# One conditioning load for each weight unit of the first SwiGLU, and the last vector's reduction near that SwiGLU's end

## The chip, the core and the metric

The kernel runs on one core of a Trainium2 chip. Time is device time of one launch in microseconds (us), and the median of the runs is compared. PE stands for the matmul engine (TensorE), DVE for VectorE, ACT for ScalarE, POOL for GpSimd, and SP for SyncE, whose queue issues all the loads here.

## What is computed

One decoder layer on 512 positions of width 1024, in fp32: a SwiGLU feed-forward (half step), a token mixer, a second SwiGLU, and a final norm. Each of the three sub-layers is conditioned: nine vectors of 1024 numbers (shift, scale and gate, three times) come from one small product of a vector `c` with a large matrix. Cut to what matters:

```python
c_act = jax.nn.silu(c)                                        # 1024
mod = (c_act @ w_ada[l] + b_ada[l]).reshape(B, 9, D_MODEL)    # w_ada: 1024 x 9216
sh1, sc1, gt1, sh2, sc2, gt2, sh3, sc3, gt3 = ...             # the nine vectors
h = _modulate(_rmsnorm(x, g_ffn1[l]), sh1, sc1)
x = x + MACARON_W * gt1 * _swiglu(h, w1_gate[l], w1_up[l], w1_down[l])
h = _modulate(_rmsnorm(x, g_mix[l]), sh2, sc2)
x = x + gt2 * _hybrid_mixer(h, ...)
h = _modulate(_rmsnorm(x, g_ffn2[l]), sh3, sc3)
x = x + MACARON_W * gt3 * _swiglu(h, w2_gate[l], w2_up[l], w2_down[l])
return _rmsnorm(x, g_final)
```

## The kernel before, in words

**Weights.** All large weights are cut into units of up to 128 x 1024 numbers (512 KB). The first SwiGLU has 68 of them (`n_ffn`): units 0 to 7 hold the first columns of gate and up, 8 to 23 and 35 to 56 the rest, 24 to 34 and 57 to 67 the two halves of down. `load_unit` (L352) loads a unit into one of four `raw` buffers from the SP queue (L356). `make_units` (L372) has ACT write its rounded part `whi` (L378), and `low_part` (L364) has DVE or POOL write the remainder `wlo` (L367) and gives the `raw` buffer back, so that the next load can go. There are four pairs of `whi` and `wlo`, and two more pairs for the last two units of a SwiGLU (`KEEP`; `whik`, `wlok` in the trace). The event `loaded[u]` is set with a unit's load, `made[u]` with its `wlo`. Each product is three matmuls, hi times hi, hi times lo and lo times hi, so a unit of eight 128 x 128 blocks is 24 matmuls of 512 columns. All of them go through the helper at L286.

**Conditioning.** The first two vectors are worked out ahead of the SwiGLU. The other seven, in the order 2, 4, 3, 5, 7, 6, 8, are worked out beside it. Each takes eight loads of 512 KB (`ada_loads`, L857, issued at L861 into one of three `araw` buffers), 56 in all. DVE multiplies each loaded tile by one column of the activated `c` and adds it to the vector's partial sums `ada` (`ada_sums`, L865; the first of eight at L875, the other seven at L878). `ada_reduce` (L885) then adds over partitions: four short matmuls on PE (L891, in the trace eight records under L286 with `ada`), a copy by ACT (L896), two transposes on PE (L899), and one or two short operations on DVE into `mod` and `am` (L902 to L912). The reduction of a vector is put in after the fourth sum of the next one (`LATER` is 3). The last vector has no next one, so its reduction comes right behind its last sum.

**Order.** A planner (`Plan`, L137) fixes the order of all instructions of every engine ahead of time. It keeps a modelled time for each engine and for the DMA queue; a step becomes ready when the events and buffers that it asks for are there in that modelled time, and the step that can start first goes first, ranks breaking ties. Each engine, and SP's queue, then runs its list strictly in that order, and waits at an instruction whose operands or buffers aren't there. The conditioning's loads and sums have rank `R_ADA` (4), the units' loads `R_LOAD` (1). The conditioning's loads ask for a free `araw` buffer and nothing else, so the planner issues the next one as soon as a sum has freed one. `glu` (L605) makes the SwiGLU's products: silu by ACT (L608), a product by DVE (L612), a rounded copy by ACT (L617), the remainder by DVE (L619). `first_half` (L638) adds the first half of down to `x`, with the gate (vector 2), at L640; `rope_tables` (L917) follows vector 4.

Of the kernel before, what the change touches and what calls it, by code (L numbers as in the profile page):

```python
# [22 lines left out]
DK = D // P  # L23
# [50 lines left out]
A_ACT = 3  # L74
HOLD = 0
N_AW = 3
LATER = 3
KEEP = (2, 2, 0)
N_PT = 4
R_H0 = 0.4  # L80
# [12 lines left out]
R_NORM, R_X, R_H, R_GLU, R_A0, R_LOAD, R_W, R_ADA, R_TAB, R_MAIN = 0, 0.5, 0.6, 0.7, 1, 2, 3, 4, 5, 9  # L93
# [43 lines left out]
class Plan:  # L137
# [12 lines left out]
    def go(self, rank, task):  # L150
        self.n += 1
        self.step([rank, self.n, task, [self.at], None], None)
# [8 lines left out]
    def give(self, slots, i, at=None):  # L161
        slots.idle.append((*(at or self.at), i))
        able = [w for w in slots.waiters if w[4] < len(slots.idle)]
        if able:
            w = min(able, key=lambda w: w[:2])
            slots.waiters.remove(w)
            self.step(w, self.take(slots, w))
# [52 lines left out]
def c_act(n):  # L220
    return ACT, 0.1 + 0.84e-3 * n
# [6 lines left out]
def c_stt(n):  # L228
    return DVE, 0.13 + 1.04e-3 * n


def c_ts(n):
    return DVE, 0.12 + 0.55e-3 * n
# [14 lines left out]
def c_dma(n):  # L248

    return DMA, max(0.05, n * 0.356e-3)  # L250
# [6 lines left out]
def tile_hymba_layer(ctx: ExitStack, tc: tile.TileContext, xT, pos, cols_d, con_d, wa0, wa1, f1a, f1b, f1d,  # L257
# [6 lines left out]
    go, give, done = plan.go, plan.give, plan.set  # L264
# [20 lines left out]
    def mm(o, lhsT, rhs, start, stop):  # L285
        nc.tensor.matmul(o, lhsT, rhs, start=start, stop=stop)  # L286
# [15 lines left out]
    def cv(n, i=0, w=1):  # L302
        a = _COLS[n][0] + i
        return col[:, a:a + w]

    def kv(n, i=0, w=None):
        a, full = _CON[n]
        return con[:, a + i:a + i + (full if w is None else w)]
# [12 lines left out]
    n_ffn = len(units)  # L321
# [20 lines left out]
    loaded, made = [Event() for _ in units], [Event() for _ in units]  # L342
# [514 lines left out]
    def ada_loads():  # L857
        for n in range(7 * DK):
            i = yield aws
            yield c_dma(4 * D)  # L860
            nc.sync.dma_start(aw[i], wa1[n // DK, n % DK])  # L861
            aw_at[n] = i
            done(aw_in[n])

    def ada_sums():  # L865
        summed = []
        for n in range(7 * DK):
            i, k = divmod(n, DK)
            yield aw_in[n]
            if k == 0:  # L870
                j = yield adas
            a, w = ada[j], aw[aw_at[n]]
            if k == 0:
                yield c_ts(D)
                nc.vector.tensor_scalar(a, w, cact[:, 0:1], None, op0=OP.mult)  # L875
            else:
                yield c_stt(D)
                nc.vector.scalar_tensor_tensor(a, w, cact[:, k:k + 1], a, op0=OP.mult, op1=OP.add)  # L878
            give(aws, aw_at[n])
            if k == DK - 1:  # L880
                summed.append((order[i], j))
            if summed and (k == LATER or n == 7 * DK - 1):
                go(R_ADA, ada_reduce(*summed.pop()))

    def ada_reduce(m, j):  # L885

        b = yield banks
        pc = bank_of[b]
        yield PE, 0.59
        for r in range(4):  # L890
            mm(pc[32 * r:32 * r + 32, :256], kv("ones"), ada[j][:, 256 * r:256 * r + 256], True, True)  # L891
        give(adas, j)
        q = yield scr
        yield c_act(256)
        t = scr_of[q]
        nc.scalar.activation(t[:, :256], pc[:, :256], AF.Copy)  # L896
        yield PE, 0.22
        for i in range(2):
            nc.tensor.transpose(pc[:, (2 + i) * P:(3 + i) * P], t[:, i * P:(i + 1) * P], ident)  # L899
        give(scr, q)  # L900
        yield SMALL
        nc.vector.tensor_add(mod[:, m].rearrange("p (r i) -> p r i", i=2),  # L902
                             pc[:, 2 * P:].rearrange("p (i r n) -> p r i n", i=2, r=4)[:, :, :, 0],
                             cv("b", m * 8, 8).rearrange("p (r i) -> p r i", i=2))
        give(banks, b)
        s, r = divmod(m, 3)
        if r == 1:
            yield SMALL
            nc.vector.scalar_tensor_tensor(am[:, s], mod[:, m], 1.0, cv(g8[s], 0, 8), op0=OP.add, op1=OP.mult)
        elif r == 2 and s != 1:  # L910
            yield SMALL
            nc.vector.tensor_scalar(mod[:, m], mod[:, m], 0.5, None, op0=OP.mult)  # L912
        done(mod_in[m])
# [51 lines left out]
    with tc.tile_pool(name="g0", bufs=1) as gp:  # L965
        go(R_ADA, ada_loads())
        go(R_ADA, ada_sums())
        go(R_TAB, rope_tables())
        parts = start_builds(1, norm)
        ffn(0, gp, accs, norm, end)  # L970
        plan.run(end)
        plan.run(mod_in[8])
        plan.run(tables_in)
# [3 lines left out]
    with ExitStack() as mixer:  # L977
# [505 lines left out]
        summed = [0] * 4  # L1483
# [134 lines left out]
        n = 0  # L1618
# [296 lines left out]
```

## Time and profile before

| | |
|---|---|
| median of 3 runs | 1060.53 us (1058.64 to 1061.17) |
| the profiled execution | 1059.17 us, of it the span 1057.4 us |
| PE busy | 1024.0 us, 97% of the span |
| DVE, ACT, POOL busy | 607.2, 409.0, 62.7 us |
| mean granted TensorE clock | 0.988 of full speed |
| HBM read | 130.14 MB, 125 GB/s over the span |

The first SwiGLU takes from about 60 us to 420 us of the span, the mixer to about 690 us, the second SwiGLU the rest. A row of the timeline gives the start, the time, the engine, the line and the operation of one instruction, and in square brackets the idle time of its engine before it and what ended that.

### The profile page before, as it was taken

Reading aid. Unit: us, or ns where it says so; the run is one execution under the profiler, and the core shown is the slowest. Engines: PE = TensorE matmul, PEld = TensorE weight load, DVE = VectorE, ACT = ScalarE, POOL = GpSimd, SP = SyncE. Lnnn points to the kernel's source line nnn. Section 1 sums busy time; section 2 is a strip of 40 time slices with the busy share of each in tenths; the row PEclk is TensorE's granted clock in tenths of the full one; section 3 lists DMA queues with packets and bytes.
Section 4 is the critical chain, followed back from the end, with each engine's and each line's share of the span. In section 5 each row is a group of like instructions: output and inputs, shape, how many; then the busy total and the mean of one; then the engine's idle time right before and its main releaser. Section 6 shows DMA issues by size and latency. Waiting matters only on the chain.

```text
span 1057.4 us, 13873 instructions
## 1 busy us (share of the span) xinstructions
PE 1024.0 (97%) x5409; PEld 859.6 (81%) x5409; DVE 607.2 (57%) x1064; ACT 409.0 (39%) x719; POOL 62.7 (6%) x52
## 2 busy tenths in 40 slices
PE   8999899899999999999999999999999999999997
PEld 5778677588888889997778778998888888888887
DVE  4988788743333345499889996654333323333334
ACT  4552222122222232356868985434322222222321
POOL 0310010000000002011121110100000000000000
PEclk8999999899999999999999999999999999999998
DMA  9659889522222230233510003224233333323202
GB/s 333 264 190 332 311 307 311 199 96 100 100 100 100 94 116 20 99 112 105 200 37 29 13 14 113 79 83 135 90 94 97 100 100 99 99 90 93 98 20 80
DMA packets 40706, 133.60 MB, mean 126 GB/s; under 512 B 4704, under 2 KB 8032, under 8 KB 40000
## 3 DMA queue, kind: packets, MB, share of 16 engines
q1 hardware_dynamic: 40640, 132.71, 37.0%
q8 instruction: 42, 0.69, 0.3%
q14 instruction: 24, 0.20, 0.1%
HBM read 130.14 MB, written 2.10 MB: 125 GB/s over the span
## 4 chain that ended last, share of the span: by engine, by line
PE 73%; DVE 13%; DMA 9%; issue 2%; ACT 2%; SPq 0%; DVEq 0%; ACTq 0%
PE b L286 71%; DMA araw<-in_wa_dram 8%; DVE ada L878 3%; DVE wlo L367 1%; DVE PT L1427 1%; PE b L1416 1%; DVE afirst L748 1%; DMA wfirst<-in_wa_dram 1%; DVE P L1344 1%; DVE s L531 1%; ACT whi L378 0%; DMA raw<-in_f1b_dram 0%; DVE q L1108 0%; DVE s L1058 0%; DVE s L612 0%
## 5 line engine op out<-in xcount | busy, mean ns | idle before, releaser
L286 PE MATMUL b<-hhi,whi 128*128 128x512 f32 (+1 forms) x1020 | 380.8, 373 | 1.4 <-DVE pc L1267 1.3
L286 PE MATMUL b<-hlo,whi 128*128 128x512 f32 (+1 forms) x1020 | 376.0, 369 | 0.8 <-DVE hlo L537 0.4
L286 PE MATMUL b<-hhi,wlo 128*128 128x512 f32 (+1 forms) x1020 | 375.5, 368 | 0.0
L378 ACT ACTIVATE whi<-raw 128x1024 fp32r<-128x1024 f32 (+3 forms) x176 | 177.9, 1012 | 444.2 <-PE b L286 296.9
L367 DVE TENSOR_TENSOR wlo<-raw,whi 128x1024 fp32r<-128x1024 f32 (+3 forms) x157 | 185.4, 1181 | 213.9 <-ACT whi L378 212.8
L286 PEld LDWEIGHTS b<-hhi,whi 128*128 128x128 f32 x1020 | 193.2, 189 | 35.3 <-issue 3.5
L286 PEld LDWEIGHTS b<-hhi,wlo 128*128 128x128 f32 x1020 | 193.2, 189 | 32.1
L286 PEld LDWEIGHTS b<-hlo,whi 128*128 128x128 f32 x1020 | 193.3, 189 | 31.5 <-DVE hlo L537 1.3
L286 PE MATMUL b<-ghi,whi 128*128 128x512 f32 (+1 forms) x364 | 137.1, 377 | 0.0
L286 PE MATMUL b<-glo,whi 128*128 128x512 f32 (+1 forms) x364 | 136.3, 374 | 0.4 <-DVE glo L619 0.4
L286 PE MATMUL b<-ghi,wlo 128*128 128x512 f32 (+1 forms) x364 | 136.2, 374 | 0.0
L612 DVE TENSOR_TENSOR s<-sg,b 128x512 f32<-128x512 f32 x44 | 30.1, 686 | 101.4 <-PE b L286 100.7
L878 DVE SCALAR_TENSOR_TENSOR ada<-araw,cact,ada 128x1024 f32<-128x1024 f32 x49 | 69.6, 1420 | 20.0 <-DMA araw<-in_wa_dram 19.6
L286 PEld LDWEIGHTS b<-ghi,whi 128*128 128x128 f32 x364 | 68.8, 189 | 13.6 <-issue 1.6
L286 PEld LDWEIGHTS b<-glo,whi 128*128 128x128 f32 x364 | 68.8, 189 | 12.8 <-DVE glo L619 0.8
L286 PEld LDWEIGHTS b<-ghi,wlo 128*128 128x128 f32 x364 | 68.8, 189 | 12.1
L367 POOL TENSOR_TENSOR wlo<-raw,whi 128x1024 fp32r<-128x1024 f32 (+2 forms) x19 | 43.9, 2311 | 286.8 <-ACT whi L378 260.7
L544 DVE SCALAR_TENSOR_TENSOR x<-b,mod,x 128x512 f32<-128x512 f32 (+1 forms) x30 | 19.1, 643 | 41.0 <-PE b L286 40.9
L462 ACT ACTIVATE s<-x 128x256 f32<-128x256 f32 (+1 forms) x41 | 19.4, 491 | 55.5 <-DVE x L544 53.7
L617 ACT ACTIVATE ghi<-s 128x512 fp32r<-128x512 f32 x44 | 27.6, 631 | 30.3 <-DVE s L612 30.3
L535 ACT ACTIVATE hhi<-s,mod 128x256 fp32r<-128x256 f32 (+1 forms) x42 | 20.9, 534 | 32.5 <-DVE s L531 29.4
L1427 DVE TENSOR_TENSOR PT<-b,PT 128x384 fp32r<-128x384 f32 (+1 forms) x48 | 28.0, 595 | 3.8 <-ACT PT L1425 3.6
(241 smaller groups left out, 963.9 us busy)
## 6 DMA issues: line engine op xcount, KB each, us to landing
araw<-in_wa_dram SPq DMA_DIRECT2D x56, 512.0 KB
raw<-in_f1b_dram SPq DMA_DIRECT2D x38, 512.0 KB
raw<-in_f2b_dram SPq DMA_DIRECT2D x38, 512.0 KB
raw<-in_f1d_dram SPq DMA_DIRECT2D x22, 512.0 KB
raw<-in_f2d_dram SPq DMA_DIRECT2D x22, 512.0 KB
raw<-in_wib_dram SPq DMA_DIRECT2D x14, 512.0 KB
wfirst<-in_wa_dram SPq DMA_DIRECT2D x5, 1024.0 KB
raw<-in_wc_dram SPq DMA_DIRECT2D x8, 512.0 KB
```

The source lines that it names most:

```text
L286: nc.tensor.matmul(o, lhsT, rhs, start=start, stop=stop)
L367: (nc.vector if e == DVE else nc.gpsimd).tensor_sub(wlo_of[j][:, :n], raw_of[i][:, :n], whi_of[j][:, :n].bitcast(F32))
L378: nc.scalar.activation(whi_of[j][:, :n], raw_of[raw_at[u]][:, :n], AF.Copy)
L462: nc.scalar.activation(o[:, ts], x[d][:, ts], AF.Square)
L531: nc.vector.scalar_tensor_tensor(t, x[d][:, ts], am[:, s, d:d + 1], rb(), op0=OP.mult, op1=OP.mult)
L535: nc.scalar.activation(hhi[d][:, ts], t, AF.Identity, bias=sh)
L544: nc.vector.scalar_tensor_tensor(x[d][:, ts], bank_of[b][:, ts], gate, x[d][:, ts], op0=OP.mult, op1=OP.add)
L612: nc.vector.tensor_mul(scr_of[q], sg_of[k], bank_of[bu])
L617: nc.scalar.activation(ghi[j], scr_of[q], AF.Copy)
L748: nc.vector.scalar_tensor_tensor(a[:, 0], w[:, k], cact[:, k:k + 1], a[:, 0], op0=OP.mult, op1=OP.add)
L878: nc.vector.scalar_tensor_tensor(a, w, cact[:, k:k + 1], a, op0=OP.mult, op1=OP.add)
L1427: nc.vector.tensor_sub(pl[:, :w], pt[:, :w], ph[:, :w].bitcast(F32))
```

## The change

The loads of the conditioning get one more condition each: load `n` is issued after the load of unit 10 + `n` of the first SwiGLU (`DK` is 8, `ADA_FROM` is 2; 56 loads, so units 10 to 65). The last vector's reduction no longer follows its last sum; it waits for the event `made` of the last unit of that SwiGLU. The other six reductions stay where they were in the order of the sums. No instruction is added or taken away. The whole diff:

```diff
-LATER = 3
+LATER, ADA_FROM = 3, 2
@@ def ada_loads
         for n in range(7 * DK):
             i = yield aws
+            yield loaded[DK + ADA_FROM + n]
             yield c_dma(4 * D)
             nc.sync.dma_start(aw[i], wa1[n // DK, n % DK])
@@ def ada_sums
             if k == DK - 1:
                 summed.append((order[i], j))
-            if summed and (k == LATER or n == 7 * DK - 1):
+            if summed and k == LATER:
                 go(R_ADA, ada_reduce(*summed.pop()))
+        yield made[n_ffn - 1]
+        go(R_ADA, ada_reduce(*summed.pop()))
```

## Rows read from the trace of the kernel before

**Rows 1.** The page, busy time of each engine over the span

```profile
PE 1024.0 (97%) x5409; PEld 859.6 (81%) x5409; DVE 607.2 (57%) x1064; ACT 409.0 (39%) x719; POOL 62.7 (6%) x52
```

**Rows 2.** Windows: stretch, busy us (instructions) of each engine, clock, DMA share, GB/s

```profile
60.00:205.00 145.00, 135.69 (x621) 106.81 (x619) 116.25 (x118) 39.84 (x54) 10.80 (x4) 0.96 0.84 294
205.00:412.00 207.00, 207.00 (x965) 173.51 (x964) 81.22 (x104) 56.58 (x70) 0.00 (x0) 1.00 0.27 93
425.00:690.00 265.00, 257.12 (x1636) 221.43 (x1636) 218.16 (x548) 171.38 (x375) 32.03 (x21) 1.00 0.24 79
```

**Rows 3.** Waits of PE, 60 to 420 us: total us, times, longest

```profile
PE b L286 <- DVE ada L878: 5.3, 1, 5.3
PE b L899 <- ACT s L896: 3.6, 1, 3.6
PE b L286 <- DVE glo L619: 0.4, 1, 0.4
```

**Rows 4.** Timeline of PE around the first long wait

```profile
113.12 0.39 PE L286 MATMUL b<-hhi,wlo 128*128 128x512 f32 x1
...
119.30 0.44 PE L899 MATMUL b<-con,s 128*128 128x128 f32 x2 [3.63 <-ACT s L896]
...
119.95 0.63 PE L286 MATMUL b<-hlo,whi 128*128 128x512 f32 x1
...
123.22 0.39 PE L286 MATMUL b<-hhi,whi 128*128 128x512 f32 x1
```

**Rows 5.** Timeline of PE around the second long wait

```profile
195.25 0.39 PE L286 MATMUL b<-ghi,wlo 128*128 128x512 f32 x1
200.91 1.08 PE L286 MATMUL b<-ada,con 128*32 128x256 f32 x8 [5.27 <-DVE ada L878]
...
205.26 0.40 PE L286 MATMUL b<-glo,whi 128*128 128x512 f32 x1
```

**Rows 6.** Timeline of PE around a reduction with no wait

```profile
187.40 0.39 PE L286 MATMUL b<-ghi,wlo 128*128 128x512 f32 x1
187.72 0.64 PE L286 MATMUL b<-ada,con 128*32 128x256 f32 x8
...
190.24 0.39 PE L286 MATMUL b<-glo,whi 128*128 128x512 f32 x1
```

**Rows 7.** Timeline of DVE and ACT inside the first long wait

```profile
115.11 2.60 DVE L878 SCALAR_TENSOR_TENSOR ada<-araw,cact,ada 128x1024 f32<-128x1024 f32 x2 [2.51 <-DMA araw<-in_wa_dram]
...
117.63 0.68 DVE L612 TENSOR_TENSOR s<-sg,b 128x512 f32<-128x512 f32 x1
...
118.34 0.63 ACT L617 ACTIVATE ghi<-s 128x512 fp32r<-128x512 f32 x1 [5.27 <-DVE s L612]
118.88 0.37 ACT L896 ACTIVATE s<-b 128x256 f32<-128x256 f32 x1
```

**Rows 8.** Waits, all engines, 60 to 205 us: DVE's sums on their loads

```profile
DVE ada L878 <- DMA araw<-in_wa_dram: 19.6, 20, 2.5
```

**Rows 9.** SP's queue: the conditioning's loads in all, then runs of unit loads

```profile
L861 SPq DMA_DIRECT2D araw<-in_wa_dram x56: 327/328/428, 66.1 to 193.8; - x56
...
210.11 103.73 SPq L356 DMA_DIRECT2D raw<-in_f1b_dram  x20
318.96 54.86 SPq L356 DMA_DIRECT2D raw<-in_f1d_dram  x11
```

**Rows 10.** Windows of 0.5 us behind the issue at 210.11: clock, DMA share, GB/s

```profile
212.00:212.50 0.50, 1.00 0.99 401
...
213.00:213.50 0.50, 1.00 0.04 16
```

**Rows 11.** Timeline: a sum on DVE beside a remainder on POOL

```profile
73.97 2.42 POOL L367 TENSOR_TENSOR wlo<-raw,whi 128x1024 fp32r<-128x1024 f32 x1 [18.27 <-ACT whi L378]
...
74.22 3.27 DVE L878 SCALAR_TENSOR_TENSOR ada<-araw,cact,ada 128x1024 f32<-128x1024 f32 x1 [0.57 <-DMA araw<-in_wa_dram]
```

**Rows 12.** The last two units' remainders: count, min/median/max ns, first and last start

```profile
L367 DVE TENSOR_TENSOR wlok<-raw,whik x2: 1216/1218/1220, 384.1 to 385.9; 128x1024 fp32r<-128x1024 f32 x2
```

## The prediction, made before the changed kernel ran

> **What bounds the kernel now.** I read the page first: PE is busy 97% of the span [rows 1], so only PE's idle or slowed time can be won. Next come the windows by stage. From 60 to 205 us, where all 56 conditioning loads run [rows 9], PE is busy 135.69 of 145 us, its mean granted clock is 0.96, the DMA engines are at 0.84 and DVE is at 116 of 145 us. From 205 to 412 us, with the same kind of matmuls and no conditioning, PE has no idle time, the clock is 1.00, DMA is at 0.27 and DVE at 81 of 207 us [rows 2]. Last, the waits of PE over both stretches: three, of 5.3, 3.6 and 0.4 us, and each ends on something that hangs on the sums [rows 3].
>
> The timeline tells why. The first wait is a chain over four engines. DVE stands 2.51 us at a sum whose load hasn't landed; behind it in DVE's order is a product of `glu` (117.63), behind that product ACT's copy for `glu` (118.34), and behind that copy, in ACT's order, the copy of a reduction (118.88), for which PE's transposes wait [rows 7]. PE stands 3.63 us [rows 4]. The second wait is the last vector's reduction. No further vector follows, so it comes right behind its last sum, and PE stands 5.27 us until that is there [rows 5]. DVE waits on the conditioning's loads 20 times in all [rows 8], but only here does it reach PE.
>
> **The change part by part.** It adds and removes no instruction: 56 loads, 56 sums and seven reductions remain, and the same bytes. It moves them.
>
> *What the two long waits cost.* An undisturbed reduction, from the matmul ahead of it to the second behind its transposes, takes 190.24 - 187.40 = 2.84 us [rows 6]. The same instructions take 205.26 - 195.25 = 10.01 us in the second wait, 7.17 us more [rows 5]. This holds the wait and the slowed matmuls behind it. In the first they take 119.95 - 113.12 = 6.83 us, 3.99 us more. Then eight matmuls take 123.22 - 119.95 = 3.27 us [rows 4]. A unit of 24 matmuls takes (103.73 - 0.33) / 19 = 5.44 us when nothing waits [rows 9], 0.227 each, so eight should take 1.81: another 1.46 us, the half clock after the wait. First wait 5.45 us, second 7.17, the small one 0.4 [rows 3]: **13.0 us** in all.
>
> *The loads, one per unit.* Units follow each other every 5.44 us [rows 9], set by PE. One unit and one conditioning load make 1.05 MB in that time, 193 GB/s, against 294 in the stretch where they crowd [rows 2]. A lone unit load, issued at 210.11, moves up to 401 GB/s and its traffic is over by about 213.3, 3.2 us after the issue [rows 10]. A second one issued behind it adds 0.524 MB at 401 to 294 GB/s, 1.3 to 1.8 us. So a pair is there after 4.5 to 5.0 us, before the next pair is issued. The first five or so loads aren't held back, because units 10 to 14 are loaded by the time the stage starts; they ran in before, too, with no wait of PE until 115 us. I take the gain of the first wait whole.
>
> *What the new condition holds up.* In SP's queue each conditioning load now stands behind a unit load, which waits for a `raw` buffer, hence for a remainder on DVE. And the next unit load stands behind the conditioning load, which waits for the sum three loads earlier, 16 us back at this pace. That is done long before, so this queue adds nothing. On DVE a sum waits for its load, and behind it are remainders and `glu`'s products. Remainders have room: four `raw` and four weight buffers lie ahead of PE, several units of 5.44 us. Products have little, as the first wait shows. Bounds for such new waits of PE: nothing at all, up to 5.45 us for each of the six reductions that stay inside the sums. I take nothing, nearest to the 18 of 20 late loads that PE never felt [rows 8].
>
> *Sums and reductions moved later.* At 5.44 us per load, some 29 of the 56 sums fall behind 205 us. At 1.30 us each [rows 7] that is 38 us more of DVE in a stretch with 81 of 207 us busy: 57%, below the 80% of the stretch they leave [rows 2]. On PE a reduction costs 2.84 us less eight matmuls, 1.03 us, in either place. The gate's vector (2) has its reduction after load 11, with unit 21, ahead of the first down unit (24), so the first half's additions don't wait. Vectors 4 and 3 and the rope tables come with units 29 and 37 of 68, well ahead of the mixer.
>
> *The last reduction.* Unit 65 is loaded 8 units after 318.96, at about 362.5, less 13 us: 349.5. Landing (5.0) and a sum (1.3) end at about 356. The last unit's remainder ended at 385.9 + 1.2 = 387.1 [rows 12], less 13: 374. The reduction asks for sums that are 18 us old, so the second wait goes, with nothing in its place there. Nothing in the mixer needs that vector.
>
> **The sum.** 1059.17 - 13.0 = 1046.1 us for the profiled execution. The median of the runs is 1.36 us above it: **1047.5 us**.
>
> **The rivals.** *A reduction still waits.* The chain of the first wait returns at one reduction or two: 1047.5 + 5.45 = 1053.0, or 1058.4 us. For it: the six reductions keep their place behind a sum, and the pattern of products, remainders and sums repeats, so one bad phase can come back. One trigger is a remainder on POOL. A sum on DVE beside one took 3.27 us instead of 1.30, a delay of 2.0 us, about the 2.51 us that set off the first wait [rows 11, 7]. Against it: between 205 and 412 us POOL had nothing to do [rows 2]. The Trainium skill, "SBUF — State Buffer", section "SBUF: two separate sides", says that VectorE and GpSimd share a pair of ports as an exclusive lock, and that the later one blocks entirely. That 3.27 us agrees. By that rule more sums beside POOL's remainders would delay DVE each time, which is this rival; should the planner keep all remainders on DVE, as it did there, the rule costs nothing.
>
> *The mixer is ordered anew.* The planner lays out the whole kernel in one go, so another order in the SwiGLU can change the choices behind it. From 425 to 690 us PE is idle 7.9 of 265 us [rows 2]. Doubled, this gives 1055.4; halved, 1043.6. Against it: the SwiGLU's last 30 us have no conditioning in either kernel except one reduction, and the mixer's start depends on them alone.
>
> *It doesn't throttle.* If the planner took the units as loaded well ahead of PE, the loads would crowd as before: 1060.5 us. Against it: unit loads need `raw` buffers and come one per 5.44 us [rows 9].
>
> *Slower.* The sums run beside 300 us of products instead of 130, and every reduction meets a DVE that stands at a load, as in rows 7. Six waits of 5.45 us are 32.7: 1080.2 us. The point from which it decides is the third wait (16.4 against 13.0 won). It needs loads that land later than their modelled time by 2.5 us each time, where DMA now is at 193 GB/s and not 294.
>
> **How the numbers follow.** Forecast 1047.5: 0.58. One wait again, 1053.0: 0.12; two, 1058.4: 0.05. Mixer worse, 1055.4: 0.08; better, 1043.6: 0.05. No throttle: 0.04. Slower by three waits or more: 0.08. A measurement of this kernel tells about 0.3%, 3.2 us, from no change. Faster: 0.58 + 0.12 + 0.08 + 0.05 = 0.83. Same: two waits and no throttle, 0.09. Slower: 0.08. The range from 1043 to 1056 holds the forecast, one wait and both mixer cases, 0.83.
>
> **What would show it.** Right: PE has no wait on `ada` or on L896 between 60 and 412 us, clock 1.00 there after the first rows; conditioning loads spread from 66 us to about 350 us, DMA near 0.55; the SwiGLU's end 13 us earlier, and all behind it shifted by as much. Wrong in the loads: DVE waits on `araw` that are as long as before, with PE standing at L899 behind them. Wrong in the mixer: more than 8 us of idle PE in its 265 us. The prediction fails most easily if the planner's place for a sum is ahead of a `glu` product whose copy stands ahead of a reduction's.

## The result and the profile after

The changed kernel takes **1046.62 us** (median of 4 runs, 1046.35 to 1046.87), against 1060.76 us for the kernel before (4 runs, 1058.64 to 1061.17). The ratio is 0.987, 95% interval 0.985 to 0.989. The forecast was 1047.5 us, the range 1043 to 1056. From profile to profile the execution went from 1059.17 to 1046.38 us, 12.8 us less, where the sum said 13.0.

The windows of the changed kernel, with the same stages as [rows 2] (the third and fourth moved by 13 us); columns as there:

```profile
60.00:205.00 145.00, 145.00 (x658) 118.19 (x657) 99.17 (x107) 42.87 (x56) 8.23 (x3) 1.00 0.57 206
205.00:399.00 194.00, 194.00 (x929) 160.34 (x928) 100.05 (x116) 53.24 (x69) 0.00 (x0) 1.00 0.47 166
...
412.00:677.00 265.00, 257.11 (x1634) 221.02 (x1633) 217.89 (x548) 171.08 (x374) 32.10 (x21) 1.00 0.25 79
```

PE is busy through all of the first two stretches, at full clock, where it had 9.3 us of idle time and a mean clock of 0.96 in the first [rows 2]. The DMA engines went from 0.84 to 0.57 and 0.47. The mixer's 265 us hold 7.9 us of idle PE in both kernels.

The waits of PE from 60 to 412 us. Of the three in [rows 3] none is left; the one shown belongs to the norm behind the SwiGLU, and the kernel before has it too:

```profile
PE b L504 <- DVE v L417: 1.2, 1, 1.2
```

The conditioning's loads and what VectorE waited for them, then a piece of SP's queue (L862 issues the conditioning's loads here, L356 the units'). The line between them gives the same waits in the kernel before:

```profile
L862 SPq DMA_DIRECT2D araw<-in_wa_dram x56: 327/424/875, 66.3 to 348.6; - x56
...
  DMA araw<-in_wa_dram: 9.0, 11
```

```profile
  DMA araw<-in_wa_dram: 24.4, 25
```

```profile
97.19 0.33 SPq L356 DMA_DIRECT2D raw<-in_f1b_dram  x1
...
97.56 0.43 SPq L862 DMA_DIRECT2D araw<-in_wa_dram  x1
...
102.63 0.33 SPq L356 DMA_DIRECT2D raw<-in_f1b_dram  x1
103.01 0.42 SPq L862 DMA_DIRECT2D araw<-in_wa_dram  x1
```

Here a pair follows the last after 5.44 us, and the last conditioning load of all is issued at 348.6 us instead of 193.8 [rows 9]. VectorE waits 9.0 us in 11 places, against 24.4 us in 25. [rows 8] has 20 of those 25, as it leaves out the waits at the first sum of a vector.

### The profile page after: what moved, and what is told of

Read it like the earlier page. It is cut to its first block, busy times and chain, and to the rows that moved or that the text cites. A ratio compares the mean times of both kernels' runs of the same rounds, so it can differ in the third digit from the quotient of the medians.

```text
span 1044.6 us, 13818 instructions
## 1 busy us (share of the span) xinstructions
PE 1018.8 (98%) x5409; PEld 856.6 (82%) x5409; DVE 608.8 (58%) x1065; ACT 408.5 (39%) x719; POOL 60.2 (6%) x51
## 4 chain that ended last, share of the span: by engine, by line
PE 84%; DVE 11%; ACT 2%; issue 1%; DMA 1%; SPq 0%; DVEq 0%; ACTq 0%
PE b L286 82%; DVE PT L1430 1%; DVE wlo L367 1%; DVE afirst L748 1%; DMA wfirst<-in_wa_dram 1%; DVE P L1347 1%; PE b L1419 1%; DVE q L1111 1%; DVE s L531 1%; ACT whi L378 0%; DVE s L1061 0%; ACT P L1351 0%; DVE swp L1064 0%; ACT P L1394 0%; DVE v L401 0%
## 5 line engine op out<-in xcount | busy, mean ns | idle before, releaser
L286 PEld LDWEIGHTS b<-ghi,whi 128*128 128x128 f32 x364 | 68.5, 188 | 12.8 <-issue 0.8
L879 DVE SCALAR_TENSOR_TENSOR ada<-araw,cact,ada 128x1024 f32<-128x1024 f32 x49 | 62.8, 1281 | 8.5 <-DMA araw<-in_wa_dram 8.1
L367 POOL TENSOR_TENSOR wlo<-raw,whi 128x1024 fp32r<-128x1024 f32 (+2 forms) x18 | 41.4, 2299 | 258.2 <-ACT whi L378 190.0
L619 DVE TENSOR_TENSOR glo<-s,ghi 128x512 fp32r<-128x512 f32 x44 | 32.2, 736 | 0.0
```

Source lines behind the costliest of these rows:

```text
L367: (nc.vector if e == DVE else nc.gpsimd).tensor_sub(wlo_of[j][:, :n], raw_of[i][:, :n], whi_of[j][:, :n].bitcast(F32))
L619: nc.vector.tensor_sub(glo[j], scr_of[q], ghi[j].bitcast(F32))
```

## The experiments

The theory: both long waits came from loads that landed late because all of them crowded into 130 us. The rivals: the place of the last reduction, the new order of the instructions, GpSimd's remainders. The kernel before was timed again beside each set: 1057.98 us (10 runs) beside the first set (e1 to e4), 1058.98 us (7 runs) beside the second (e5 to e8). The ratio of every run is to the one of its own set.

### One part alone: the loads (e1_rate_only)

```diff
# against the changed kernel
-            if summed and k == LATER:
+            if summed and (k == LATER or n == 7 * DK - 1):
                 go(R_ADA, ada_reduce(*summed.pop()))
-        yield made[n_ffn - 1]
-        go(R_ADA, ada_reduce(*summed.pop()))
```

> The loads are tied to the units as in the changed kernel, but the last vector's reduction comes right behind its last sum, as in the kernel before. If late loads are what made both long waits, timely loads leave little of the second one: PE waits for at most the lag of one landing behind its modelled time, some 1.5 us, and 1046.6 becomes 1047 to 1049 us. If the second wait (7.17 us) belongs to the place of the reduction, whatever the loads do, it stays: 1053.8 us. The first wait (5.45 us) is gone by both.

Measured: 1047.01 us, ratio 0.990 (0.987 to 0.992). The wait of PE at the last reduction is gone, although the reduction is back behind its last sum. VectorE's last sums and PE's reduction (the `x8` row), then PE's transposes:

```profile
351.42 1.28 DVE L879 SCALAR_TENSOR_TENSOR ada<-araw,cact,ada 128x1024 f32<-128x1024 f32 x1 [1.94 <-DMA araw<-in_wa_dram]
...
354.17 1.28 DVE L879 SCALAR_TENSOR_TENSOR ada<-araw,cact,ada 128x1024 f32<-128x1024 f32 x1
```

```profile
356.76 0.64 PE L286 MATMUL b<-ada,con 128*32 128x256 f32 x8
...
358.83 0.38 PE L900 MATMUL b<-con,s 128*128 128x128 f32 x2
```

VectorE stood 1.94 us at one load, yet the last sum ended at 355.45, 1.3 us before PE came to it at 356.76. So the loads alone carry the gain. What the moved reduction adds to them (1047.01 against 1046.62, measured in another set) can't be told from nothing by these runs.

### The other part alone: the last reduction (e2_last_only)

```diff
# against the kernel before
-            if summed and (k == LATER or n == 7 * DK - 1):
+            if summed and k == LATER:
                 go(R_ADA, ada_reduce(*summed.pop()))
+        yield made[n_ffn - 1]
+        go(R_ADA, ada_reduce(*summed.pop()))
```

> The loads crowd as in the kernel before; only the last vector's reduction waits for the last unit of the SwiGLU. If the terms of the sum stand by themselves, the second wait's 7.17 us go and the first wait's 5.45 and the small one's 0.4 stay: 1060.8 - 7.2 = 1053.6 us. If the crowded loads find another place to hold PE up once this one is taken away, 1057 to 1061 us. If the reduction's place was the whole of it, 1047 us.

Measured: 1050.66 us against 1057.98, 7.3 us less; ratio 0.993 (0.991 to 0.995). The difference is the one expected, 7.2 us, but the time is 2.9 us below the 1053.6 that were expected. The first wait is still where it was, shorter, and nothing slow follows it. PE around it, and two small waits before the first product of the down half:

```profile
118.52 0.44 PE L901 MATMUL b<-con,s 128*128 128x128 f32 x2 [2.83 <-ACT s L898]
118.71 0.48 PE L286 MATMUL b<-hhi,whi 128*128 128x512 f32 x1
119.02 0.39 PE L286 MATMUL b<-hlo,whi 128*128 128x512 f32 x1
119.25 0.39 PE L286 MATMUL b<-hhi,wlo 128*128 128x512 f32 x1
...
169.75 0.49 PE L286 MATMUL b<-ghi,whi 128*128 128x512 f32 x1 [0.28 <-ACT ghi L617]
170.82 0.50 PE L286 MATMUL b<-glo,whi 128*128 128x512 f32 x1 [0.58 <-DVE glo L619]
```

2.83 + 0.28 + 0.58 = 3.7 us of the 3.9 by which this kernel's span (1048.5) exceeds that of the changed one (1044.6). Up to 140 us the order is the same on every engine and in SP's queue here, in the kernel before and in e3 below. So their first wait is one wait seen in three executions: 3.63, 2.83 and 2.61 us. The 5.45 us that the prediction put on it were the price of one execution. The parts don't add up: 11.0 us for the loads alone, 7.3 for the reduction alone, 12.7 for both in the second set (1046.3 against 1058.98, below). Each removes the second wait by itself.

### The order of before, with loads that land early (e4_half_bytes)

```diff
# against the kernel before
-            nc.sync.dma_start(aw[i], wa1[n // DK, n % DK])
+            nc.sync.dma_start(aw[i][:, :D // 2], wa1[n // DK, n % DK][:, :D // 2])
-            a, w = ada[j], aw[aw_at[n]]
+            a = ada[j].rearrange("p (k n) -> p k n", k=2)
+            w = aw[aw_at[n]][:, :D // 2].unsqueeze(1).to_broadcast([P, 2, D // 2])
```

> The kernel before with every instruction in the same order on every engine, but each conditioning load brings only the first half of its tile (256 KB), and its sum reads that half twice, so that the sums take as long as before; the second half of each conditioning row is left out of what is computed. If late landing made the waits, the first one goes (5.45), the small one too, and of the second (7.17) only what lies between the sum and the reduction stays, 0 to 4 us: 1047 to 1052 us. If the order of the instructions made them, they stay: 1058 to 1061 us.

Measured: 1045.88 us, ratio 0.989 (0.986 to 0.991), 1.1 us below the range expected. All instructions stand where the kernel before has them; only the bytes differ. PE's waits (60 to 412 us), VectorE's waits on the loads, and the window of the crowded stretch:

```profile
PE b L504 <- DVE v L417: 1.2, 1, 1.2
```

```profile
DVE ada L876 <- DMA araw<-in_wa_dram: 2.2, 2, 1.8
```

```profile
60.00:205.00 145.00, 145.00 (x679) 115.75 (x678) 128.00 (x137) 43.22 (x59) 10.98 (x4) 1.00 0.63 202
```

VectorE is busier than before (128 of 145 us, against 116 in [rows 2]). It waits 2.2 us on the loads, where the kernel before waited 24.4. PE never waits on the conditioning. Even the last reduction, right behind its last sum, costs nothing. In this order, late landing made the waits; neither VectorE's load nor the place of the reduction did.

### The order of after, with loads that land late (e6_loads_late)

```diff
# against the changed kernel
             nc.sync.dma_start(aw[i], wa1[n // DK, n % DK])
+            nc.sync.dma_start(aw[i], wa1[n // DK, n % DK])
```

> The changed kernel with the same order of instructions on PE, VectorE, ScalarE and GpSimd, but each conditioning load is issued twice into the same buffer, the second behind the first's landing, so that a tile is there some 3 us later and the stretch carries 1.57 MB per 5.44 us (289 GB/s). If late landing makes the waits, whatever the order, VectorE's waits on these loads grow from 9 us to 40 or more and PE waits at two to six of the reductions, 2 to 5.5 us each: 1051 to 1075 us. If the new order is what keeps PE fed, the time stays at 1046.6, within 2.

Measured: 1132.67 us, ratio 1.070 (1.068 to 1.072). The direction is the one the theory asks for, but the size is far outside: the delay that I put in was larger than I thought. SP's own waits and PE's, 60 to 400 us, and the window of the stretch:

```profile
SPq L863 <- DMA araw<-in_wa_dram: 249.6, 50, 6.6
```

```profile
PE b L903 <- ACT s L900: 35.9, 4, 12.5
PE b L286 <- DVE wlo L367: 8.5, 2, 5.3
PE b L286 <- DVE glo L619: 5.3, 1, 5.3
PE b L286 <- ACT ghi L617: 2.8, 1, 2.8
```

```profile
60.00:205.00 145.00, 114.51 (x476) 91.19 (x476) 64.35 (x71) 32.98 (x47) 7.25 (x3) 0.90 0.64 230
```

The second load of a pair waits in SP's queue for the first to land, 5.0 us each time (249.6 / 50), and the next unit's load stands behind it. I had counted the later landing and not the held queue. So this run shows that the new order doesn't protect PE from late loads, and that PE waits most at the reductions' transposes (L903, 36 of 53 us). It waits at remainders and products too. The stretch carries only 230 GB/s, so the loads are late here without being crowded. The run doesn't give the price of a landing 3 us late, which stays open.

### How many loads per unit (e3_two_per_unit, e7_three_per_two, e8_after_again)

```diff
# against the changed kernel: e3, then e7; e8 is the changed kernel itself
-            yield loaded[DK + ADA_FROM + n]
+            yield loaded[DK + ADA_FROM + n // 2]
+            yield loaded[DK + ADA_FROM + 2 * n // 3]
```

> The changed kernel with two conditioning loads for each unit (load n behind unit 10 + n // 2), so they end with unit 37. That is 1.57 MB per 5.44 us, 289 GB/s, near the 294 of the crowded stretch of before. If the rate of the loads is what matters, VectorE's waits on them come back to 15 to 25 and PE gets one or two of the waits of 5.45 us: 1052 to 1058 us. If it is enough that each load is tied to a unit, 1046.6 us, within 2.

> Three conditioning loads for two units (load n behind unit 10 + 2n // 3): 1.31 MB per 5.44 us, 241 GB/s, between the 193 of one per unit and the 289 of two. If the waits come with the rate, this lies between the two: no wait or one, 1046.6 to 1050 us. If they hang on the phase in which a sum meets a product and a reduction, it may be worse than two per unit: over 1052 us.

> The changed kernel once more, beside the others on one chip: 1046.6 us, and a spread of its runs under 1.5 us by every theory. If the spread of before (5 us) comes from crowded loads, the kernels with 241 and 289 GB/s spread by 1 to 5 us in this same call; if it comes from the chip, this one spreads as well.

Measured: two per unit 1052.0 us (1050.8 to 1055.8), ratio 0.994 (0.993 to 0.996), in the first set. Three per two units 1046.38 us, ratio 0.988 (0.987 to 0.990), and one per unit 1046.3 us, 0.988 (0.987 to 0.990), both in the second set. The windows from 60 to 205 us of two per unit and of three per two:

```profile
60.00:205.00 145.00, 140.21 (x651) 111.91 (x651) 121.91 (x135) 42.60 (x59) 4.89 (x2) 1.00 0.83 294
```

```profile
60.00:205.00 145.00, 145.00 (x663) 117.63 (x664) 110.77 (x120) 44.01 (x58) 8.30 (x3) 1.00 0.72 258
```

With two per unit PE waits again, at the transposes of two reductions:

```profile
119.15 0.44 PE L902 MATMUL b<-con,s 128*128 128x128 f32 x2 [2.61 <-ACT s L899]
119.35 0.48 PE L286 MATMUL b<-hhi,whi 128*128 128x512 f32 x1
119.66 0.39 PE L286 MATMUL b<-hlo,whi 128*128 128x512 f32 x1
...
156.29 0.44 PE L902 MATMUL b<-con,s 128*128 128x128 f32 x2 [2.18 <-ACT s L899]
```

That is 4.8 us, and the time is 5.4 us over one per unit. At 258 GB/s in the stretch there is no such wait, at 294 there are two. VectorE's waits on the loads are 21.0 us with two per unit (15 to 25 were expected), 13.0 with three per two. Its sums ahead of the two waits of PE:

```profile
114.96 2.61 DVE L879 SCALAR_TENSOR_TENSOR ada<-araw,cact,ada 128x1024 f32<-128x1024 f32 x2 [2.00 <-DMA araw<-in_wa_dram]
...
151.89 1.28 DVE L879 SCALAR_TENSOR_TENSOR ada<-araw,cact,ada 128x1024 f32<-128x1024 f32 x1 [0.56 <-DMA araw<-in_wa_dram]
```

The first wait is the chain of [rows 7] again. Ahead of the second VectorE stood 0.56 us at a load and otherwise worked almost without a break from 142.06 us on, so there the work that crowds on VectorE counts as well as the late load. The forecast for two per unit was 1052 to 1058 us with one or two waits; it came at the lower end, since each wait was half as dear as the one it was priced by. So it isn't the tie to a unit that helps, but the rate it sets. These kernels differ in order too, so the point between 258 and 294 GB/s holds for them alone, and e6 shows that loads can be late at 230 GB/s. On the spread of the runs: the changed kernel spread by 1.3 us (under 1.5 was expected) and three per two by 0.8 (1 to 5 was expected, if crowding makes it). Two per unit spread by 5 us and the kernel before by 2.5 to 5, but e2, whose loads crowd as much, by 0.6 only. What makes the spread stays open.

### Remainders on GpSimd (e5_pool_remainders)

```diff
# against the changed kernel, in low_part
-        e = yield c_tt(n), (*c_ptt(n), POOL_TAX)
+        if DK + ADA_FROM <= u < n_ffn and u % 2:
+            e = yield c_ptt(n)
+        else:
+            e = yield c_tt(n), (*c_ptt(n), POOL_TAX)
```

> The changed kernel with every second remainder of units 10 to 67 put on GpSimd by hand (44 remainders there in all instead of 17). If GpSimd's remainders can bring the first wait's chain back, sums and products beside them take some 2 us longer on VectorE, and PE waits at one reduction or more, 5.45 us each, most often in the six that stay among the sums: 1052 us (one) to 1079 us (six). If the room that one load per unit leaves takes those 2 us, PE has no wait before 390 us and the time stays at 1046.6, within 2.

Measured: 1046.18 us, ratio 0.988 (0.987 to 0.990), with no wait of PE on the conditioning. VectorE's waits on the loads (60 to 400 us), a remainder on POOL, and two sums, the first of them beside it:

```profile
DVE ada L882 <- DMA araw<-in_wa_dram: 38.6, 29, 3.4
...
DVE ada L879 <- DMA araw<-in_wa_dram: 9.5, 5, 3.3
```

```profile
101.49 2.43 POOL L370 TENSOR_TENSOR wlo<-raw,whi 128x1024 fp32r<-128x1024 f32 x1 [8.43 <-ACT whi L381]
...
102.25 2.75 DVE L882 SCALAR_TENSOR_TENSOR ada<-araw,cact,ada 128x1024 f32<-128x1024 f32 x1 [0.97 <-DMA araw<-in_wa_dram]
...
108.94 1.28 DVE L882 SCALAR_TENSOR_TENSOR ada<-araw,cact,ada 128x1024 f32<-128x1024 f32 x1 [0.83 <-DMA araw<-in_wa_dram]
```

The sum beside GpSimd takes 1.5 us longer (2.0 in [rows 11]). The Trainium skill, "SBUF — State Buffer", section "SBUF: two separate sides", calls the shared ports an exclusive lock, where the later of the two instructions blocks fully. The trace agrees: the sum ends 1.1 us after the remainder, and takes 1.28 us without one. But it costs PE nothing. And VectorE waits 38.6 us here at the sums that waited 19.6 us in the kernel before [rows 8], with no wait of PE. So a wait of VectorE on a load says little by itself. It did harm where PE soon needed what stood behind it: a product and a reduction's copy in the first wait, the last reduction in the second, remainders and products in e6. What spared PE in e5 was not followed wait by wait.

## Why the prediction was right

**The terms of the sum.** 13.0 us were predicted and 12.8 came, from profile to profile. The rows named beforehand came out close: no wait on `ada` or at the transposes, clock 1.00, loads until 348.6 us (about 350 was said), DMA at 0.57 and 0.47 (near 0.55), the same 7.9 us of idle PE in the mixer. The median was put 1.36 us above the profiled execution, as before; it was 0.24 above. The reduction of the last vector and the remainders that it waits for:

```profile
L286 PE MATMUL b<-ada,con x56: 379/391/404, 110.6 to 374.1; 128*32 128x256 f32 x56
```

```profile
L367 DVE TENSOR_TENSOR wlok<-raw,whik x2: 1212/1215/1218, 369.9 to 371.7; 128x1024 fp32r<-128x1024 f32 x2
```

The last remainder ended at 372.9 (374 was said), and the last sum, which began at 353.6 and took 1.28, at 354.9 (356).

**The landing of a pair** was put at 4.5 to 5.0 us. A conditioning load of the changed kernel and the sum that waited for it:

```profile
116.00 0.43 SPq L862 DMA_DIRECT2D araw<-in_wa_dram  x1
```

```profile
120.89 1.28 DVE L879 SCALAR_TENSOR_TENSOR ada<-araw,cact,ada 128x1024 f32<-128x1024 f32 x1 [0.92 <-DMA araw<-in_wa_dram]
```

That is 4.9 us from its own issue and some 5.3 from the unit's load ahead of it, a little over the bound and still under 5.44. The forecast took waits of this size on VectorE as harmless, and they were.

**Where the reasoning was less exact.** The second wait was credited to the moved reduction alone. e1 shows that the loads alone remove it too, and e2 that the reduction alone does; the moved reduction is spare. The sum holds all the same, since each wait was counted once. That it met the profiled pair to 0.2 us is partly chance, because the first wait changes from one execution to the next (3.63, 2.83 and 2.61 us, see e2), and the medians give 14.1 us here and 12.7 in the second set. That the six reductions keep some risk was right in kind: with two loads per unit two of them wait again. The price of 5.45 us for such a wait was too high for those: 2.2 to 2.6 us, with no slow matmuls behind. VectorE's waits on the loads were 25 in all, not 20. Its share behind 205 us was put at 57% and came at 52% (100.05 of 194 us): 28 sums moved there as counted, but the rope tables and four remainders moved out of it.

**The rivals.** A reduction that still waits did not show, nor any change in the mixer's idle time. The rate rivals (no throttle; three waits or more) needed loads that crowd or come late. e3 crowded them again and brought two waits, e6 made them late and brought four at the reductions by 400 us. The trigger named for the first rival, a remainder on POOL, was tried by e5 and costs nothing in that order.

## What to carry to other kernels

When an engine off the critical path works through loads in strict order, look at what is queued behind its waits: here 2.5 us of one late load passed over a product and two copies to the matmul engine, while most of the other waits on loads (25 in all) did nothing. Background loads should be paced by the work that they run beside, at a rate under what the DMA engines carried when crowded (here 206 GB/s or 258 instead of 294), and not by how soon a buffer comes free. The rate is the means and an early landing the end: in e6 the loads came late at 230 GB/s. Moving the step that consumes them late is a second guard, and was worth nothing that could be measured where the first held.

## What the runs showed of the hardware

After waits of 3.63 and 5.27 us, PE's next matmuls ran at half speed (0.43 us apart instead of 0.227), and the granted clock was 0.85 in the 10 us from 120 us on:

```profile
120.38 0.63 PE L286 MATMUL b<-hhi,wlo 128*128 128x512 f32 x1
120.81 0.63 PE L286 MATMUL b<-hhi,whi 128*128 128x512 f32 x1
```

```profile
120.00:130.00 10.00, 10.00 (x39) 8.10 (x38) 7.38 (x10) 2.13 (x3) 0.00 (x0) 0.85 0.89 308
```

After the waits of 2.18, 2.61 and 2.83 us in e3 and e2 they ran at full speed from the first on, and the granted clock stayed at 1.00. The same window in e2:

```profile
120.00:130.00 10.00, 10.00 (x46) 8.28 (x45) 8.02 (x9) 2.61 (x3) 1.85 (x1) 1.00 0.94 317
```

So the wait of 3.63 us cost another 1.46 us behind it, and that of 2.83 us in e2 nothing. The length of the wait alone doesn't decide it. In e6, 11 us after a wait of 7.36 us, another wait of 2.83 us was followed by a granted clock of 0.50 and a matmul that took 0.80 us:

```profile
196.69 0.80 PE L286 MATMUL b<-ghi,whi 128*128 128x512 f32 x1 [2.83 <-ACT ghi L617]
```

```profile
196.70:201.00 4.30, 0.78 (x1) 0.27 (x1) 0.12 (x1) 0.88 (x1) 0.00 (x0) 0.50 0.50 157
```

A very small VectorE instruction can be held by GpSimd as long as a large one. In the changed kernel one on 128 x 8 numbers, 0.17 us elsewhere, took 2.38 us beside a remainder of 2.44 us on POOL:

```profile
113.16 2.44 POOL L367 TENSOR_TENSOR wlo<-raw,whi 128x1024 fp32r<-128x1024 f32 x1 [35.64 <-ACT whi L378]
```

```profile
113.24 2.38 DVE L915 TENSOR_SCALAR mod<-mod 128x8 f32<-128x8 f32 x1
```
